# Reordering the first ten projection jobs of a hybrid decoder block, and two more jobs as seven block products

## The chip, the cores and the metric

The kernel runs on one core of a Trainium2 chip. The metric is the device time of one execution in microseconds (us), less being better. TensorE is called PE, VectorE DVE, ScalarE ACT, GpSimd POOL; SP issues most DMAs. PEld is PE's loading of stationary operands, which overlaps its matmuls.

## The reference, cut to what matters

One layer, 256 tokens, width 2048, float32. Cut to the matrix products:

```python
h = rms_norm(x, norm_mix_pre)
p, q, k, v, g_lr, r, gate_logits = split(h @ w_in)          # 1024 1024 1024 2048 16 2048 4096 columns
y_a = pool_mixer(p, w_pool, pool_scale) @ w_branch_a
log_a = log_sigmoid(g_lr @ w_gate_up + b_gate) / 16
o = gla_chunked(q, k, v, log_a)                             # 4 heads, chunks of 64 tokens
o = rms_norm(o, gla_norm) * silu(r)
y_b = o @ w_branch_b
gates = sigmoid(gate_logits + b_branch_gates)
x = x + rms_norm((gates[0] * y_a + gates[1] * y_b) @ w_out, norm_mix_post)
h = rms_norm(x, norm_ffn_pre)
f = (silu(h @ w_ffn_gate) * (h @ w_ffn_up)) @ w_ffn_down    # 5632 columns in between
x = x + rms_norm(f, norm_ffn_post)
```

## The kernel before, in words

**Jobs and steps.** All weight products are a list of 68 jobs, written by `plan()` (L63). A job makes 512 columns of one product for all 256 tokens (two tiles of 128 tokens). Its name is a kind and a number: p0 and p1 are the columns of p, r0 to r3 those of r (r0 also holds the 16 columns of g_lr), and so on; down (2,1) is the second 512 columns of the third part of w_ffn_down, which has 12 tiles of 128 rows where the other jobs have 16 (or 8, for branch a). A plain job goes through its rows in steps of two such tiles. For each step SP loads 512 KB (L334), ACT rounds the weights to a first part `wh` (L343) and DVE computes the rest `wl` (L347). Activations are kept in the same two parts. PE then multiplies three times for each tile of rows and each tile of tokens: first part by first part, first by rest, rest by first (L381 to L383 with 512 columns each; L365 to L367 where the output is wanted transposed, for p, q and k).

**Block jobs.** Where the last value that `plan()` yields is true, the first eight tiles of rows (a 1024 x 512 block) are multiplied with seven products in place of eight: the block is cut into 2 x 2 blocks of 512 x 256, and sums of them are multiplied with sums of the activations' blocks. The seven products are called q1, r5, q6, q7 (these four may run early) and q2, q4, r3. Each has four tiles of rows and one tile of tokens: 12 matmuls of 256 columns (L441 to L443). The sums cost DVE three adds of 128 x 1024 (L402, L404, L406) and POOL one adding DMA (L413); every product has its own `wh` (ACT, L417) and `wl` (DVE, L421) of 128 x 1024. ACT copies running sums out of PSUM (L445, L450, L452) and DVE subtracts (L453). The rest of the rows goes in steps as in a plain job, but as two matmuls of 256 columns instead of one of 512. The activations' sums come from `combine` (L247 on), whose pieces are run as background work.

**What sets the order.** `merged` (L297) weaves the four early products of a block job between the last units of the job ahead of it. A scheduler then places the instructions in each engine's queue when the program is built; each queue runs in order. The limits are pools: four buffers each for `wh` and `wl` (BUFS), three for loaded rows (RAWS), three for blocks of 1 MB (BLOCKS), and eight tiles of 512 columns in PSUM, called banks here. Four (`acc`) hold two jobs' outputs. The other four (`tr`) serve transposes and small products; a block job takes two of them for its running sums (`j.a`, `j.c` in `Part.multiply`, L432), and r0, with its 528 columns, takes two for the whole job beside two of `acc` (`j.extra` in `Step.multiply`, L350).

**Work that hangs on these jobs.** When p0 and p1 end, DVE runs the pooling (L540 to L561) and PE small products with w_pool (L570). When an r job ends, ACT takes silu of it and stores it to DRAM (L586 to L591, `r_done`). r0 also starts the gate chain: the weights of the gate (L603 to L608), the product (L630, L631), then Abs, Exp and Ln on ACT (L636, L639, L643), each over two tiles of 128 x 1024, with a subtraction on DVE (L644). Exp and Ln and silu need other tables in ACT (ACT_TABLE_LOAD). When k1 ends, the levels of the gated attention begin as background work beside the jobs a0 to a3 and v0. At the end of the kernel the third part of down is fed by `f2`, whose third group is transposed on PE (L204) right after up10 and split into `f22h` (ACT, L240) and `f22l` (DVE, L241).

Where rows of an order are shown below, the lines of the changed kernel stand one higher than here from L71 on.

Of the kernel before, what the change touches and what calls it, by code (L numbers as in the profile page):

```python
# [22 lines left out]
RANK = 16  # L23
# [3 lines left out]
CW = 512  # L27
# [26 lines left out]
OFF_P, OFF_Q, OFF_K, OFF_V, OFF_G, OFF_R, OFF_GA = 0, 1024, 2048, 3072, 5120, 5136, 7184  # L54
# [8 lines left out]
def plan():  # L63

    kt = D // P
    for kind, off, order in [("p", OFF_P, (0, 1)), ("r", OFF_R, (1, 2, 3, 0)), ("q", OFF_Q, (0, 1)), ("k", OFF_K, (0, 1))]:
        for i in order:
            low = kind == "r" and i == 0
            yield (kind, i, "w_in", 0, kt, OFF_G if low else off + i * CW, CW + RANK if low else CW,
                   kind == "r" and i > 1)  # L70
    for n in range(4):  # L71
        yield "a", n, "w_branch_a", 0, kt // 2, n * CW, CW, False
    for n in range(4):
        yield "v", n, "w_in", 0, kt, OFF_V + n * CW, CW, n > 0
    for n in range(8):
        yield "gates", n, "w_in", 0, kt, OFF_GA + n * CW, CW, n != 3
    for n in range(4):
        yield "b", n, "w_branch_b", 0, kt, n * CW, CW, n in (1, 3)
    for n in range(4):
        yield "out", n, "w_out", 0, kt, n * CW, CW, n < 3  # L80
    chunks = DFF // CW
    for part in range(3):
        ms = range(part * 4, min(part * 4 + 4, chunks))
        for m in ms:
            yield "gate", m, "w_ffn_gate", 0, kt, m * CW, CW, m > 0
            yield "up", m, "w_ffn_up", 0, kt, m * CW, CW, m > 0
        for n in range(4):
            yield "down", (part, n), "w_ffn_down", part * 16, 4 * len(ms), n * CW, CW, (part, n) not in ((2, 1), (2, 3))


def packed(name, w):

    import numpy as np

    out = []
    for _, _, which, k0, kt, c0, width, fast in plan():
        if which != name:
            continue
        rows = w[0, k0 * P:(k0 + kt) * P, c0:c0 + width].reshape(kt, P, width)
        if fast:  # L100
            for b in range(2):
                blocks = rows[b * 4:b * 4 + 4].reshape(4, P, 2, HW)
                out.append(blocks.transpose(2, 1, 0, 3).ravel())
            rows = rows[4 * FAST:]
        out.append(rows.reshape(-1, GK, P, width).transpose(0, 2, 1, 3).ravel())
    return np.concatenate(out)
# [3 lines left out]
def tile_hybrid_block(ctx: ExitStack, tc: tile.TileContext, *aps):  # L110
# [925 lines left out]
    for kind, n, name, k0, kt, c0, width, fast in plan():  # L1036
        jobs.append(Job(source[name], at[name], kt, width, fast, **kinds[kind](n)))
        at[name] += kt * P * width
# [132 lines left out]
```

## Time and profile before

| | |
|---|---|
| median of 3 runs (lowest, highest) | 1462.31 us (1461.0, 1462.92) |
| the profiled execution | 1462.98 us, its span 1461.2 us |
| PE busy | 1441.4 us (99%) |
| DVE busy | 1230.7 us (84%) |
| ACT busy | 905.0 us (62%) |
| POOL busy | 70.5 us (5%) |
| DMA | 315.50 MB, mean 216 GB/s |
| granted PE clock | 0.999 |

The span runs from the first to the last instruction; the time holds 1.78 us more around it. Busy shares are averages over stages with different limits. PE's records overlap, as matmuls are pipelined: what a matmul costs in a stream is the distance from its start to the next one's.

### The profile page before, as it was taken

To read this page: it belongs to the slowest core of one execution; us is meant where nothing else is said; L and a number is where in the kernel's file an instruction comes from. 1 tells how busy PE (TensorE), PEld (TensorE's weight loads), DVE (VectorE), ACT (ScalarE), POOL (GpSimd) and SP (SyncE) were. 2 spreads that over 40 slices of the span, in tenths; PEclk is the share of its full clock that TensorE was granted. 3 is DMA by queue.
4 is the path that set the end of the run, shared out by engine and by line. 5 is a ranking of instruction groups with operands and counts; after the bars stand their busy time and mean duration, and the time that the engine had idled before them with its cause. 6 is when DMAs were issued, how large, how long until landed. Compare 5 with 4: busy or idle time off the path is not lost.

```text
span 1461.2 us, 27921 instructions
## 1 busy us (share of the span) xinstructions
PE 1441.4 (99%) x11344; PEld 1380.4 (94%) x11344; DVE 1230.7 (84%) x1382; ACT 905.0 (62%) x1183; POOL 70.5 (5%) x95
## 2 busy tenths in 40 slices
PE   8999999999999999999999999999999999999997
PEld 8999999889999999999978999999999999999986
DVE  6785568898998997799778899988889899889986
ACT  6465735556775665566557666666666666666654
POOL 2000000000100000000000000000000000000000
PEclk9999999999999999999999999999999999999999
DMA  8746566726768578649854767777776777777644
GB/s 291 259 136 219 194 211 213 234 90 214 225 201 275 183 251 265 216 150 292 271 169 165 219 221 228 219 227 236 231 223 215 225 230 226 231 238 229 203 166 145
DMA packets 89345, 315.50 MB, mean 216 GB/s; under 512 B 10188, under 2 KB 10912, under 8 KB 88960
## 3 DMA queue, kind: packets, MB, share of 16 engines
q1 hardware_dynamic: 77616, 278.89, 55.8%
q0 software_dynamic: 8304, 29.11, 10.5%
q10 hardware_dynamic: 3296, 5.71, 1.1%
q8 instruction: 89, 1.46, 0.4%
q14 instruction: 40, 0.33, 0.1%
HBM read 284.84 MB, written 4.19 MB: 198 GB/s over the span
## 4 chain that ended last, share of the span: by engine, by line
PE 83%; DVE 8%; issue 3%; DMA 2%; ACT 2%; SPq 0%; POOL 0%; DVEq 0%; ACTq 0%; POOLq 0%
PE acc L381 15%; PE acc L383 15%; PE acc L382 15%; PE ac L441 5%; PE ac L442 5%; PE ac L443 5%; PE acc L443 4%; PE acc L442 4%; PE acc L441 4%; PE acc L367 3%; PE acc L366 3%; PE acc L365 3%; DVE wl L421 2%; DVE wl L347 2%; DMA raw<-in_w_in_dram 2%
## 5 line engine op out<-in xcount | busy, mean ns | idle before, releaser
L343 ACT ACTIVATE wh<-raw 128x1024 fp32r<-128x1024 f32 (+1 forms) x332 | 351.4, 1059 | 285.7 <-PE acc L383 122.3
L347 DVE TENSOR_TENSOR wl<-raw,wh 128x1024 fp32r<-128x1024 f32 (+1 forms) x332 | 405.6, 1223 | 104.4 <-ACT wh L343 101.6
L421 DVE TENSOR_TENSOR wl<-blocks,wh 128x1024 fp32r<-128x1024 f32 x329 | 399.4, 1221 | 76.9 <-ACT wh L417 75.2
L417 ACT ACTIVATE wh<-blocks 128x1024 fp32r<-128x1024 f32 x329 | 346.0, 1059 | 152.6 <-PE acc L383 64.0
L441 PE MATMUL ac<-wh,x 128*128 128x256 f32 x420 | 116.8, 278 | 0.4 <-ACT wh L417 0.4
L442 PE MATMUL ac<-wl,x 128*128 128x256 f32 x420 | 116.2, 277 | 0.0
L443 PE MATMUL ac<-wh,x 128*128 128x256 f32 x420 | 116.1, 277 | 0.0
L382 PE MATMUL acc<-wl,h22h 128*128 128x256 f32 (+1 forms) x336 | 95.3, 284 | 1.6 <-DVE wl L347 1.6
L381 PE MATMUL acc<-wh,h22h 128*128 128x256 f32 (+1 forms) x336 | 95.8, 285 | 0.0
L381 PE MATMUL acc<-wh,h23h 128*128 128x256 f32 (+1 forms) x336 | 94.7, 282 | 0.5 <-ACT wh L343 0.5
L383 PE MATMUL acc<-wh,h22l 128*128 128x256 f32 (+1 forms) x336 | 94.8, 282 | 0.0
L383 PE MATMUL acc<-wh,h23l 128*128 128x256 f32 (+1 forms) x336 | 94.7, 282 | 0.0
L382 PE MATMUL acc<-wl,h23h 128*128 128x256 f32 (+1 forms) x336 | 94.6, 282 | 0.0
L413 POOL DMA_DIRECT2D blocks<-blocks x47 | 40.7, 866 | 883.0 <-DVE blocks L402 154.6
L441 PEld LDWEIGHTS ac<-wh,x 128*128 128x128 f32 x420 | 78.8, 188 | 1.1 <-ACT wh L417 0.6
L442 PEld LDWEIGHTS ac<-wl,x 128*128 128x128 f32 x420 | 78.9, 188 | 0.5
L443 PEld LDWEIGHTS ac<-wh,x 128*128 128x128 f32 x420 | 78.9, 188 | 0.0
L382 PEld LDWEIGHTS acc<-wl,h22h 128*128 128x128 f32 x336 | 63.1, 188 | 2.9 <-DVE wl L347 2.4
L382 PE MATMUL acc<-wl,h2h 128*128 128x256 f32 (+2 forms) x224 | 65.1, 291 | 0.4 <-DVE wl L347 0.4
L381 PE MATMUL acc<-wh,h2h 128*128 128x256 f32 (+2 forms) x224 | 65.1, 291 | 0.0
L383 PE MATMUL acc<-wh,h2l 128*128 128x256 f32 (+2 forms) x224 | 64.9, 290 | 0.0
L382 PE MATMUL acc<-wl,h3h 128*128 128x256 f32 (+2 forms) x224 | 64.7, 289 | 0.0
(549 smaller groups left out, 4614.9 us busy)
## 6 DMA issues: line engine op xcount, KB each, us to landing
raw<-in_w_in_dram SPq DMA_DIRECT2D x120, 512.0 KB, 4.2
blocks<-in_w_in_dram SPq DMA_DIRECT2D x48, 512.0 KB, 4.5
raw<-in_w_ffn_gate_dram SPq DMA_DIRECT2D x48, 512.0 KB, 4.4
raw<-in_w_ffn_up_dram SPq DMA_DIRECT2D x48, 512.0 KB, 4.3
raw<-in_w_ffn_down_dram SPq DMA_DIRECT2D x48, 512.0 KB, 4.4
blocks<-blocks POOLq DMA_DIRECT2D x47, 512.0 KB, 5.8
blocks<-in_w_ffn_gate_dram SPq DMA_DIRECT2D x40, 512.0 KB, 4.3
blocks<-in_w_ffn_up_dram SPq DMA_DIRECT2D x40, 512.0 KB, 4.4
```

The source lines that it names most:

```text
L343: act.activation(self.hi, self.raw, AF.Copy)
L347: dve.tensor_tensor(self.lo, self.raw, f32(self.hi), op=ALU.subtract)
L365: pe.matmul(dst, wh, ah, start=first and c % 2 == 0, stop=False)
L366: pe.matmul(dst, wl, ah, start=False, stop=False)
L381: pe.matmul(ps, ah, hi[:, i, cs], start=first and begins, stop=False, skip_group_check=loose)
L382: pe.matmul(ps, ah, lo[:, i, cs], start=False, stop=False, skip_group_check=loose)
L383: pe.matmul(ps, al, hi[:, i, cs], start=False, stop=last and ends, skip_group_check=loose)
L417: act.activation(self.hi, self.src, AF.Copy)
L421: dve.tensor_tensor(self.lo, self.src, f32(self.hi), op=ALU.subtract)
L441: pe.matmul(dst, ah, wh, start=i == 0 and p in ("q1", "r5"), stop=False, skip_group_check=True)
L442: pe.matmul(dst, ah, wl, start=False, stop=False, skip_group_check=True)
L443: pe.matmul(dst, al, wh, start=False, stop=i == 3 and p in EARLY, skip_group_check=True)
```

## The change

Two rules of `plan()` change. The first ten jobs were p0 p1 r1 r2 r3 r0 q0 q1 k0 k1; now they are p0 p1 r0 r1 q0 r2 q1 r3 k0 k1, and r1 becomes a block job as r2 and r3 are. In down's third part the second job, down (2,1), becomes a block job too; the last, down (2,3), stays plain. The packing of the weights in DRAM follows the same plan on the host.

```diff
-    for kind, off, order in [("p", OFF_P, (0, 1)), ("r", OFF_R, (1, 2, 3, 0)), ("q", OFF_Q, (0, 1)), ("k", OFF_K, (0, 1))]:
-        for i in order:
-            low = kind == "r" and i == 0
-            yield (kind, i, "w_in", 0, kt, OFF_G if low else off + i * CW, CW + RANK if low else CW,
-                   kind == "r" and i > 1)
+    first = {"p": OFF_P, "r": OFF_R, "q": OFF_Q, "k": OFF_K}
+    for kind, i in zip("pprrqrqrkk", (0, 1, 0, 1, 0, 2, 1, 3, 0, 1)):
+
+        low = kind == "r" and i == 0
+        yield (kind, i, "w_in", 0, kt, OFF_G if low else first[kind] + i * CW, CW + RANK if low else CW,
+               kind == "r" and i > 0)
...
-            yield "down", (part, n), "w_ffn_down", part * 16, 4 * len(ms), n * CW, CW, (part, n) not in ((2, 1), (2, 3))
+            yield "down", (part, n), "w_ffn_down", part * 16, 4 * len(ms), n * CW, CW, (part, n) != (2, 3)
```

**PE, the early product r5 of the first block r job.** Before, that job is r2, and its r5 (into the running sum `ac_128_933`) stands between the two small products with w_pool, with half of r1 (`acc_112`, `acc_113`) still ahead:

```order
L383 MATMUL acc_113_833<-wh_118_871,h2l_127 128x512
L570 MATMUL tr_137_974<-qt_120_887,scr_136_972 128x256 [waits DMAHW1_49,DVE_49]
L570 MATMUL tr_137_974<-qt_120_887,scr_136_972 128x256 x3
L441 MATMUL ac_128_933<-wh_121_897,x_74_557 128x256 [waits Activation_49]
L442 MATMUL ac_128_933<-wl_122_899,x_74_557 128x256 [waits DVE_49]
L443 MATMUL ac_128_933<-wh_121_897,x_75_558 128x256
```

Now it is r1, and its r5 (into `ac_129_980`) stands behind the last matmuls of r0, whose four banks are `acc_111`, `acc_112`, `tr_113` and `tr_114`:

```order
L384 MATMUL tr_113_831<-wh_145_1098,h3l_128 128x264
L382 MATMUL acc_112_830<-wh_145_1098,h3h_124 128x264
L383 MATMUL acc_112_830<-wl_146_1100,h3h_124 128x264
L384 MATMUL acc_112_830<-wh_145_1098,h3l_128 128x264
L382 MATMUL tr_114_832<-wh_145_1098,h3h_124 128x264
L383 MATMUL tr_114_832<-wl_146_1100,h3h_124 128x264
L384 MATMUL tr_114_832<-wh_145_1098,h3l_128 128x264
L442 MATMUL ac_129_980<-wh_122_932,x_74_557 128x256 [waits Activation_49]
L443 MATMUL ac_129_980<-wl_123_934,x_74_557 128x256
```

r5 has moved to the end of the job ahead of it, and its first matmul waits for ACT: the instruction that it waits for is ACT's silu of `tr_113`, whose bank `ac_129` takes over.

**DVE, down's third part.** Before, these rows follow the last product of down (2,0), which is `wl_2287`; `wl_2290` is its last step, `wl_2294` and `wl_2298` are the first two steps of the plain job (2,1), `wl_2300` is the early q1 of (2,2), and `ff0`, `ff1` are the outputs of (2,0):

```order
L421 TENSOR_TENSOR wl_2287_16392<-blocks_2248_16093,wh_2286_16390 128x1024
L347 TENSOR_TENSOR wl_2290_16410<-raw_2288_16406,wh_2289_16408 128x1024
L241 TENSOR_TENSOR f22l_15308<-tr_2291_16412,f22h_15304 128x512
L241 TENSOR_TENSOR f22l_15308<-tr_2295_16449,f22h_15304 128x512
L347 TENSOR_TENSOR wl_2294_16447<-raw_2292_16443,wh_2293_16445 128x1024
L347 TENSOR_TENSOR wl_2298_16472<-raw_2296_16468,wh_2297_16470 128x1024
L421 TENSOR_TENSOR wl_2300_16488<-blocks_2258_16179,wh_2299_16486 128x1024
L997 SCALAR_TENSOR_TENSOR ff0_10852<-acc_2264_16206,rstd2_1223_8686,ff0_10852 128x512
L997 SCALAR_TENSOR_TENSOR ff1_10854<-acc_2265_16207,rstd2_1223_8686,ff1_10854 128x512
```

Now `wl_2296` is the last product of (2,0); `blocks_2263` and `blocks_2292` are the blocks of (2,1), `wl_2304` and `wl_2310` its q6 and q7; `wl_2308` and `wl_2313` are the two steps of (2,0):

```order
L422 TENSOR_TENSOR wl_2296_16515<-blocks_2256_16201,wh_2295_16513 128x1024
L403 TENSOR_TENSOR blocks_2263_16255<-blocks_2263_16255,blocks_2292_16467 128x1024
L242 TENSOR_TENSOR f22l_15416<-tr_2298_16520,f22h_15412 128x512
L242 TENSOR_TENSOR f22l_15416<-tr_2305_16548,f22h_15412 128x512
L422 TENSOR_TENSOR wl_2304_16546<-blocks_2263_16255,wh_2303_16544 128x1024
L405 TENSOR_TENSOR blocks_2263_16255<-blocks_2263_16255 128x1024
L348 TENSOR_TENSOR wl_2308_16573<-raw_2306_16569,wh_2307_16571 128x1024
L422 TENSOR_TENSOR wl_2310_16589<-blocks_2263_16255,wh_2309_16587 128x1024
L348 TENSOR_TENSOR wl_2313_16607<-raw_2311_16603,wh_2312_16605 128x1024
L454 TENSOR_TENSOR acc_2301_16529<-ac_2300_16528,u_2314_16621 128x256
```

The steps of (2,0), whose matmuls read `f22h` and `f22l`, have moved behind four early products of (2,1), and two block sums have come in between.

**ACT, the gate chain.** Before, Abs (L636), Exp (L639) and Ln (L643) stand among the `wh` of plain jobs:

```order
L636 ACTIVATE S0_1881<-P0_1879 128x1024
L639 ACT_TABLE_LOAD
L639 ACTIVATE S0_1881<-S0_1881 128x1024
L343 ACTIVATE wh_263_1965<-raw_262_1963 128x1024
L636 ACTIVATE S1_1882<-P1_1880 128x1024
L343 ACTIVATE wh_266_1996<-raw_265_1994 128x1024
L639 ACTIVATE S1_1882<-S1_1882 128x1024
L643 ACT_TABLE_LOAD
```

Now they stand behind r1's silu (L590) and among the `wh` of q0 (L344) and of r2's early products (L418):

```order
L590 ACTIVATE scr_185_1430<-acc_131_982,rstd0_55_440 128x512
L344 ACTIVATE wh_187_1436<-raw_186_1434 128x1024
L592 DMA r11_1432<-scr_185_1430 128x512
L640 ACT_TABLE_LOAD
L640 ACTIVATE S0_1275<-S0_1275 128x1024
L418 ACTIVATE wh_191_1467<-blocks_141_1058 128x1024
L640 ACTIVATE S1_1276<-S1_1276 128x1024
L344 ACTIVATE wh_194_1498<-raw_193_1496 128x1024
L644 ACT_TABLE_LOAD
```

The chain has moved from plain jobs to the job that carries r2's early products; the silus of r2 and r3 now come after it, and ACT's queue holds nine table loads instead of seven. From k0 to up10 PE's queue is the same as before, and the other queues differ in a few places that lie one or two rows apart and in one more table load at the first level of the attention.

## Rows read from the trace of the kernel before

**Rows 1.** The page: busy time (share of the span) and instructions of each engine.
```profile
PE 1441.4 (99%) x11344; PEld 1380.4 (94%) x11344; DVE 1230.7 (84%) x1382; ACT 905.0 (62%) x1183; POOL 70.5 (5%) x95
```
**Rows 2.** PE's waits: who waited for whom: us in total, times, longest.
```profile
PE acc L382 <- DVE wl L347: 2.0, 3, 0.9
...
PE acc L381 <- ACT h20h L243: 0.8, 3, 0.4
PE acc L381 <- ACT f22h L240: 0.8, 1, 0.8
PE acc L383 <- DVE f22l L241: 0.6, 1, 0.6
...
PE ac L441 <- ACT wh L417: 0.4, 1, 0.4
```
**Rows 3.** PE's timeline: start, us, instruction, count [idle before]; 22 matmuls, then 12.
```profile
69.67 0.39 PE L383 MATMUL acc<-wh,h1l 128*128 128x512 f32 x1
...
74.47 0.39 PE L383 MATMUL acc<-wh,h1l 128*128 128x512 f32 x1
74.70 0.28 PE L441 MATMUL ac<-wh,h0h 128*128 128x256 f32 x1
...
75.95 0.28 PE L443 MATMUL ac<-wh,h0l 128*128 128x256 f32 x1
```
**Rows 4.** PE's timeline at the early products of r3.
```profile
104.16 0.39 PE L381 MATMUL acc<-wh,h2h 128*128 128x256 f32 x2
105.00 0.38 PE L441 MATMUL ac<-wh,x 128*128 128x256 f32 x1 [0.45 <-ACT wh L417]
105.22 0.28 PE L382 MATMUL acc<-wl,h2h 128*128 128x256 f32 x1
```
**Rows 5.** PE's timeline at the first step of down (2,0).
```profile
1392.38 0.28 PE L441 MATMUL acc<-wh,f21h 128*128 128x256 f32 x1
...
1393.79 1.04 PE L204 MATMUL tr<-ident,scr 128*128 128x128 f32 x8
1395.63 0.39 PE L381 MATMUL acc<-wh,f22h 128*128 128x256 f32 x1 [0.80 <-ACT f22h L240]
...
1396.10 0.28 PE L382 MATMUL acc<-wl,f22h 128*128 128x256 f32 x1
1397.01 0.38 PE L383 MATMUL acc<-wh,f22l 128*128 128x256 f32 x1 [0.63 <-DVE f22l L241]
```
**Rows 6.** ACT's timeline where r0 ends.
```profile
153.34 0.27 ACT L586 ACTIVATE glow<-acc,rstd 128x16 f32<-128x16 f32 x1 [0.76 <-PE acc L383]
153.51 0.46 ACT L589 ACTIVATE scr<-acc,rstd 128x248 f32<-128x248 f32 x1
153.86 0.48 ACT L589 ACTIVATE scr<-tr,rstd 128x264 f32<-128x264 f32 x1
```
**Rows 7.** ACT's timeline in the gate chain.
```profile
166.19 1.28 ACT L639 ACT_TABLE_LOAD   x1
167.49 1.06 ACT L639 ACTIVATE S<-S 128x1024 f32<-128x1024 f32 x1
168.46 1.04 ACT L343 ACTIVATE wh<-raw 128x1024 fp32r<-128x1024 f32 x1
```
**Rows 8.** DVE's timeline: a stretch without idle time, and the last part of down.
```profile
78.79 1.22 DVE L347 TENSOR_TENSOR wl<-raw,wh 128x1024 fp32r<-128x1024 f32 x1
79.92 1.22 DVE L404 TENSOR_TENSOR blocks<-blocks 128x1024 f32<-128x1024 f32 x1
81.06 1.22 DVE L421 TENSOR_TENSOR wl<-blocks,wh 128x1024 fp32r<-128x1024 f32 x1
...
1387.29 0.43 DVE L453 TENSOR_TENSOR acc<-ac,u 128x256 f32<-128x256 f32 x1
1387.62 1.22 DVE L421 TENSOR_TENSOR wl<-blocks,wh 128x1024 fp32r<-128x1024 f32 x1
```
**Rows 9.** Busy time by stretch: us, PE PEld DVE ACT POOL, clock, DMA share, GB/s.
```profile
63.60:94.50 30.90, 30.90 (x163) 26.56 (x162) 28.35 (x45) 16.74 (x22) 0.95 (x1) 1.00 0.46 133
131.00:154.20 23.20, 23.20 (x194) 23.20 (x193) 10.48 (x9) 10.24 (x13) 0.00 (x0) 1.00 0.70 232
154.20:199.50 45.30, 45.30 (x396) 45.05 (x395) 29.91 (x35) 29.12 (x33) 1.92 (x2) 1.00 0.62 206
```
**Rows 10.** The same over 1387.3 to 1436.6 us: the row of sums.
```profile
sum 49.30, PE 47.86 PEld 44.43 DVE 40.45 ACT 28.18 POOL 1.13; mean PE 11.97 PEld 11.11 DVE 10.11 ACT 7.04 POOL 0.28
```
**Rows 11.** DMA issues: count, KB each, median us from issue to landing.
```profile
raw<-in_w_ffn_down_dram SPq DMA_DIRECT2D x48, 512.0 KB, 4.4
blocks<-blocks POOLq DMA_DIRECT2D x47, 512.0 KB, 5.8
...
wgu<-in_w_gate_up_dram ACTq DMA_DIRECT2D x3, 64.0 KB, 2.0
```

## The prediction

> **What bounds the kernel now.** I read the page's busy line first. PE is busy for 99% of the span, DVE for 84% [rows 1]. That alone does not say that PE is the bound everywhere, so I read PE's waits next: the longest entry of PE waiting for DVE's `wl` is 2.0 us in three waits, the others are below 1 us [rows 2]. So PE's stream is the path, and the kernel gets shorter by what leaves that stream and longer by each new hole in it. DVE is the engine to watch for holes: while r1 and the early products of r2 ran, from 63.6 to 94.5 us, DVE was busy 28.35 of 30.90 us, but only 10.48 of 23.20 in r0 and 29.91 of 45.30 in q0 and q1 [rows 9]. In the last part of down, from 1387.3 to 1436.6 us, it was busy 40.45 of 49.30 [rows 10].
>
> All sums below are made against the profiled execution, 1462.98 us, which is 0.67 us above the median of the runs shown, 1462.31. About 0.2% of that, 2.9 us, is what a measurement of this kernel can tell from no change.
>
> **PE's stream: -3.0 us.** Matmuls of 512 columns start 4.80 us / 21 = 0.2286 us apart, those of 256 columns 1.25 / 11 = 0.1136 [rows 3]. A plain r job is 8 steps x 2 x 2 x 3 = 96 of the long ones, 21.95 us. As a block job it is 7 x 12 = 84 short ones and 4 steps x 24 = 96 short ones, 180 in all, 20.45 us: -1.50. Down (2,1) falls from 6 x 12 = 72 long ones, 16.46 us, to 84 + 48 = 132 short ones, 15.00 us: -1.46. Moving a job past another costs PE nothing in itself.
>
> **What the two jobs cost the others.** Seven products stand in place of four steps, so each of the two jobs gives ACT and DVE three more pieces of 128 x 1024, DVE three block sums and two subtractions, and POOL one adding DMA. On DVE a piece takes 1.13 to 1.14 us from start to start and a subtraction 0.33 [rows 8]: 6 x 1.135 + 2 x 0.33 = 7.5 us a job. The bytes loaded stay the same; SP's queue issues 512 KB pieces as before, whose landing takes 4.4 us, and the adding DMA 5.8 us [rows 11].
>
> **A hole that goes near 105 us: -0.7 us.** r3's q6 had to wait for its `wh` there: two matmuls from 104.16 would have ended by 104.39, the next began at 105.00, and the one after it 0.22 instead of 0.11 us later [rows 4]. DVE was late because two block jobs followed each other while the pooling was still being worked off. Now r3's early products lie between steps of q1, which are 24 matmuls long, and the pooling is long over.
>
> **The wait that r1's r5 gets: +1.4 us.** r5's running sum takes over a bank of r0, so its first matmul waits for ACT's silu of that bank, and r5 stands directly behind r0's last matmul. Everything on PE waits with it. ACT cannot start on r0 before the last matmul into `acc_111`, the tenth from the end: some 1.05 us before r0's stream ends, and it is there at about 0.9, as u and `wh` of r1's s4 stand ahead. Then come the copy of g_lr, 0.17 to the next start, a table load, 1.30, silu of 248 columns, 0.35, and silu of 264 columns, 0.48 [rows 6, 7]: 2.3 us, so r5 is let go 1.4 us after it could run. Bounds: 0.9 if ACT starts the moment it can and the table load overlaps something, 2.8 if ACT is a piece of 1.06 us later. What is queued behind r5 on PE waits too; on DVE the two subtractions of r1 wait for r5, but they have 3 us to spare. For the gate's weights behind them, the chain of a memset, a DMA of 2.0 us [rows 11] and two pieces ends some 2.5 us before PE wants them; that is their cover.
>
> The ScalarE page of the Trainium skill ("ScalarE: Activation LUTs", section "What ACT_TABLE_LOAD costs") says that a switch of tables costs 1283 ns and a drain of some 1380 ns, 2.66 us together, and asks that work be grouped by table, which this change undoes for silu. The load is 1.28 us here too, but the trace shows the next instruction 0.02 us behind it [rows 7], so I price a switch at 1.30; by the page r5's wait would be 2.8 us.
>
> **Small lateness in the new front: +0.6 us (0 to 2).** DVE's order puts a block sum ahead of the `wl` of r0's s5, and r5 no longer stands before that step on PE. Summing DVE's rows from 58.2 us on, with the prices above, `wl` is there 0.3 us after PE wants it: +0.3. In q0, the two Exp, two Ln and the silus of r1 lie between the `wh` of q0 and of r2's early products. Two table loads at 1.30 and some ten pieces at 0.95 to 0.97 [rows 7] from r1's end bring Ln's end to 12.6 us after it; then a piece of 1.2 and a block sum lead to the `wl` of q0's s5, wanted 16.4 us after r1's end: I get 0.3 us late, +0.3. Two more table loads lie in ACT's idle time (q0 and q1 had 29.12 of 45.30 us of it busy [rows 9]) and cost nothing.
>
> **The end: -1.8 us and +2.7 us.** Before, down (2,0) had its first step as second unit, right behind the transposes of up10's last group. The eight transposes begin at 1393.79, at 0.11 us each PE was free at 1394.66, the step began at 1395.63; then from 1396.10 to 1397.01 it waited again for `f22l` [rows 5]: 0.97 + 0.80 = 1.8 us. Now q4, r3 and three early products of (2,1) stand ahead of that step, 5 x 1.36 = 6.8 us of cover: both waits go.
>
> What is late next is DVE. It enters with a lead: (2,0)'s q2 began on PE at 1392.38, while its `wl` was done at 1388.84 [rows 5, 8]. From 1387.62 on I count DVE's order up to the `wl` of (2,2)'s q6: 21 pieces at 1.135, six of half size at 0.60, two outputs at 0.66, three subtractions at 0.33, 29.7 us, so it is done at 1417.4. PE without a hole gets there after 12 units of 12 matmuls, two of 24 and the transposes, 16.3 + 5.4 + 0.9 = 22.6 us after 1392.38, at 1415.0, and wants `wl` 0.1 us later. So PE loses 2.3 us by then, mainly at r5 and q6 of (2,2); with 0.4 us for pieces that wait for ACT, +2.7. Behind that point the plain job (2,3) gives DVE its slack back. Lower bound 0.5, if DVE keeps more of its lead; upper bound the whole 7.5 us, if none of DVE's idle time can be used.
>
> **Sum.** -3.0 - 0.7 + 1.4 + 0.6 - 1.8 + 2.7 = -0.8: 1462.2 us for the profiled execution, **1461.5 us** for the median.
>
> **The rivals.** *The holes stay small.* DVE keeps its lead in down (+0.5), the front is not late (0), r5's wait is 0.9: -3.0 - 0.7 + 0.9 - 1.8 + 0.5 = -4.1, 1458.2. For it: DVE has 8.85 us of idle time in the end [rows 10], more than the 7.5 it gets. Against it: products of 1.36 us on PE need 1.14 us of DVE each, and the block sums and outputs come on top. Chance 0.22.
>
> *Slower: DVE becomes the bound of down's third part.* Weight pieces are made at most four units ahead of PE, and an early product has PE's time for 12 matmuls alone, so DVE's idle time may be of no use; then all 7.5 us appear on PE: -0.8 + 4.8 = +4.0, 1466.3. It decides where the `wl` of (2,1)'s s4 comes more than 2 us after PE's end of q6. For it: in three block jobs of 15 us in a row DVE has 12 pieces, two subtractions and two outputs in two passes each, 16.8 us a job. Against it: the third of them is followed by a plain job, and the first enters with the lead of 3.5 us. Chance 0.12.
>
> *Slower: a table switch costs far more than its row.* At 2.7 us a switch, r5's wait doubles (+1.4) and the two loads in q0 add 2.8 to the lateness of q0's s5: +3.4, 1465.7. The rows show nothing behind a load but 0.02 us [rows 7]: chance 0.03. This is the case that the ScalarE page of the Trainium skill would make.
>
> That the block jobs are not made where the change puts them is excluded by the order shown.
>
> **How the numbers follow.** The forecast has a chance of 0.63. It lies within 0.2%, the first rival is faster by 4.1 us, the other two are slower by over 2.9. So faster 0.22, same 0.63, slower 0.15. The range reaches down to the first rival's time and up to near the two slower ones, which leaves out about 2 in 10: 1458.0 to 1465.5. The forecast's own range is 1459.5 to 1464.5.
>
> **What would show it.** Right: r1 takes 180 matmuls of 256 columns; one hole of about 1.4 us directly before r1's r5, ended by ACT's silu; no hole at r3's q6; no wait for `f22h`; some 2 to 3 us of PE waiting for `wl` in (2,1) and the early products of (2,2). Wrong: holes in r2 or r3, DMA landings that end waits in down's third part, or PE waiting for DVE in down for more than 5 us or less than 1.

## The result and the profile after

The changed kernel takes 1464.91 us in the median of 12 runs (1463.81 to 1467.08), the kernel before 1462.16 beside it (12 runs). The ratio is 1.0019, 95% interval 1.0011 to 1.0027: a loss of 2.75 us where 0.8 us of gain was forecast. The time lies inside the range on record, at its upper end; the sign was wrong.

The profiled execution of the changed kernel took 1464.67 us, its span is 1462.9. Its busy line, beside [rows 1]:

```profile
PE 1441.2 (99%) x11488; PEld 1386.5 (95%) x11488; DVE 1244.8 (85%) x1398; ACT 917.2 (63%) x1199; POOL 72.6 (5%) x97
```

PE has 144 matmuls more and is busy for as long as before, though the short matmuls of two jobs were to save 3 us. DVE has 14 us more and ACT 12, as counted (7.5 a job on DVE).

PE's waits in the changed kernel (who waited for whom, us in total, times, longest), beside [rows 2]:

```profile
...
PE acc L383 <- DVE wl L348: 1.6, 2, 0.9
PE ac L442 <- ACT scr L590: 1.5, 1, 1.5
PE acc L382 <- ACT wh L344: 1.1, 2, 0.6
...
PE ac L442 <- ACT wh L418: 0.6, 1, 0.6
PE acc L367 <- DVE wl L348: 0.5, 1, 0.5
...
PE ac L442 <- DVE f22l L242: 0.4, 1, 0.4
...
PE acc L442 <- DVE acc L454: 0.3, 1, 0.3
```

The forecast wait is there (silu, L590, 1.5 us), the wait for `f22h` is gone, that for `f22l` is 0.4 and in another place. But the new waits together do not make the loss. To see where it lies I cut both spans at the same places of the program, by the start of the first matmul of a job:

| from ... to | before | after | difference |
|---|---|---|---|
| start to the first r job | 63.72 | 63.62 | -0.1 |
| first r job to a0 | 179.33 | 182.71 | +3.4 |
| a0 to down (2,0), its q1 | 1132.21 | 1130.89 | -1.3 |
| down (2,0), its q1, to down (2,3) | 61.36 | 61.09 | -0.3 |
| the last job and what is behind it | 24.6 | 24.6 | 0.0 |

The third line is no work of the change: PE's instructions there are the same, and over the runs below that leave its banks as they are this stretch took from 1131.0 to 1132.4 us, with the old front and with the new. So the change costs some 3.4 us in the first ten jobs and gives 0.3 back in down. The first of these stretches, and k0 with k1 inside it, by windows: the stretch, its length, busy time of PE, PEld, DVE, ACT, POOL with instruction counts (a window also counts what overlaps its ends), granted clock, DMA share, GB/s. The kernel before:

```profile
63.72:243.05 179.33, 178.88 (x1444) 174.05 (x1443) 123.39 (x141) 98.70 (x112) 3.18 (x4) 1.00 0.58 190
199.53:243.05 43.52, 43.52 (x386) 43.52 (x385) 28.05 (x30) 18.41 (x18) 0.00 (x0) 1.00 0.59 197
```

The changed kernel:

```profile
63.62:246.33 182.71, 180.39 (x1529) 179.25 (x1528) 130.17 (x148) 105.14 (x120) 3.72 (x4) 1.00 0.57 187
201.09:246.33 45.24, 45.24 (x387) 45.24 (x386) 26.56 (x27) 20.19 (x21) 0.00 (x0) 1.00 0.66 214
```

The second line of each is the surprise. k0 and k1 are 384 matmuls of 256 columns in both kernels, in the same order, with no idle time in either and the clock at its upper level (1.00). They take 43.52 us before and 45.24 after: 0.1133 and 0.1178 us from start to start. PE's timeline of the changed kernel where r3 ends and k0 begins (start, us, instruction, count):

```profile
200.41 0.28 PE L382 MATMUL acc<-wh,h3h 128*128 128x256 f32 x1
...
201.09 0.28 PE L366 MATMUL acc<-h0h,wh 128*128 128x256 f32 x1
...
202.28 0.28 PE L367 MATMUL acc<-h0h,wl 128*128 128x256 f32 x1
```

Six matmuls of r3 take 0.68 us, the ten of k0 behind them 1.19. From the first matmul of k0 on PE goes 4% slower, with nothing waited for, for 45 us. I call this PE's pace. Sorting all distances between successive starts on PE from the first r job to a0 by size gives the whole: distances up to 0.13 us for 256 columns (0.245 for 512) are pace, what is above is a hole. Matmul columns at the fast pace (0.1133 us for each 256): -1.4; holes: 3.1 before, 5.0 after, +1.9; pace: 0.9 before, 3.8 after, +2.9. Sum +3.4.

### The profile page after: what moved, and what is told of

The parts are those of the page before. It is cut to its first block, busy times and chain, and to the rows that moved or that the text cites. A ratio compares the mean times of both kernels' runs of the same rounds, so it can differ in the third digit from the quotient of the medians.

```text
span 1462.9 us, 28244 instructions
## 1 busy us (share of the span) xinstructions
PE 1441.2 (99%) x11488; PEld 1386.5 (95%) x11488; DVE 1244.8 (85%) x1398; ACT 917.2 (63%) x1199; POOL 72.6 (5%) x97
## 3 DMA queue, kind: packets, MB, share of 16 engines
q8 instruction: 90, 1.47, 0.4%
## 4 chain that ended last, share of the span: by engine, by line
PE 85%; DVE 6%; issue 3%; ACT 2%; DMA 2%; SPq 0%; POOL 0%; DVEq 0%; ACTq 0%; POOLq 0%
PE acc L382 15%; PE acc L383 15%; PE acc L384 15%; PE ac L442 5%; PE ac L443 5%; PE ac L444 5%; PE acc L442 4%; PE acc L444 4%; PE acc L443 4%; PE acc L368 2%; PE acc L367 2%; PE acc L366 2%; DVE wl L422 2%; DMA raw<-in_w_in_dram 2%; DVE wl L348 1%
## 5 line engine op out<-in xcount | busy, mean ns | idle before, releaser
L344 ACT ACTIVATE wh<-raw 128x1024 fp32r<-128x1024 f32 (+1 forms) x324 | 343.0, 1059 | 265.1 <-PE acc L384 109.2
L422 DVE TENSOR_TENSOR wl<-blocks,wh 128x1024 fp32r<-128x1024 f32 x343 | 416.0, 1220 | 79.0 <-ACT wh L418 77.1
L348 DVE TENSOR_TENSOR wl<-raw,wh 128x1024 fp32r<-128x1024 f32 (+1 forms) x324 | 395.3, 1222 | 87.0 <-ACT wh L344 84.2
L418 ACT ACTIVATE wh<-blocks 128x1024 fp32r<-128x1024 f32 x343 | 360.9, 1059 | 165.4 <-PE acc L384 65.8
L442 PE MATMUL ac<-wh,x 128*128 128x256 f32 x432 | 120.0, 278 | 1.5 <-ACT scr L590 1.5
L443 PE MATMUL ac<-wl,x 128*128 128x256 f32 x432 | 119.7, 277 | 0.0
L444 PE MATMUL ac<-wh,x 128*128 128x256 f32 x432 | 119.6, 277 | 0.0
L442 PEld LDWEIGHTS ac<-wh,x 128*128 128x128 f32 x432 | 81.1, 188 | 2.1 <-ACT scr L590 1.7
L444 PEld LDWEIGHTS ac<-wh,x 128*128 128x128 f32 x432 | 81.2, 188 | 0.0
L384 PE MATMUL acc<-wh,h3l 128*128 128x256 f32 (+2 forms) x232 | 66.0, 285 | 0.0
```

The costliest lines, as they stand in the source:

```text
L344: act.activation(self.hi, self.raw, AF.Copy)
L348: dve.tensor_tensor(self.lo, self.raw, f32(self.hi), op=ALU.subtract)
L384: pe.matmul(ps, al, hi[:, i, cs], start=False, stop=last and ends, skip_group_check=loose)
L418: act.activation(self.hi, self.src, AF.Copy)
L422: dve.tensor_tensor(self.lo, self.src, f32(self.hi), op=ALU.subtract)
L442: pe.matmul(dst, ah, wh, start=i == 0 and p in ("q1", "r5"), stop=False, skip_group_check=True)
```

## The experiments

Two theories. **A**: PE has two paces for the same matmuls, a state that lasts until something in its stream disturbs it, and the new order of jobs puts q1's first steps, k0 and k1 into the slower one. **B**: the loss is the new holes, and the pace is a matter of the single execution.

**e1_front, e2_order, e3_r1, e4_down** take the change apart.

```diff
 e1_front (of the changed kernel)
-... (part, n) != (2, 3)
+... (part, n) not in ((2, 1), (2, 3))
 e2_order: as e1_front, and
-... kind == "r" and i > 0
+... kind == "r" and i > 1
 e3_r1 (of the kernel before)
-... kind == "r" and i > 1
+... kind == "r" and i > 0
 e4_down (of the kernel before)
-... (part, n) not in ((2, 1), (2, 3))
+... (part, n) != (2, 3)
```

> The new order with r1 as a block job, but down (2,1) plain as before. Theory A (pace): matmuls of 256 columns start either 113.3 or 117.8 ns apart, the state lasts over many jobs, and the new order, in which q and k jobs follow block jobs, puts q1, k0 and k1 into the slower one. Then k0 and k1 run at 117.8 again, the stretch from r0 to a0 is about 183 us as in the changed kernel, and the time is 2.5 to 3.5 us above before. Theory B (waits): the holes that the change makes are the loss, and the pace is a matter of the single execution. Then k0 and k1 are as likely at 113.3, and the time is 1 to 2 us above before.

> The new order alone: r1 and down (2,1) stay plain. Theory A: q1, k0 and k1 at 117.8 ns although no job has changed its form, 2 to 3 us above before. Theory B: no wait before r1's r5, since there is none; the hole at r3's q6 gone (-0.7), q0's s5 late (+0.7): the time of before, within 0.5 us.

> The old order p0 p1 r1 r2 r3 r0 q0 q1 k0 k1 with r1 as a block job; down as before. Theory A: q0 to k1 follow the plain job r0 as before and stay at 113.3 ns; r1 saves 1.3 us of matmuls, and its early products fall into p1, where DVE also has the pooling: new holes of 1 to 3 us there; 0 to 2 us above before. Theory B: the same holes, so the same time, and k0 and k1 at either pace.

> Old order, r1 plain, only down (2,1) as a block job. Both theories: in down's third part the two waits for f22h and f22l go (-1.8), the early products of (2,2) wait for their weights (+2), matmuls -1.3: 0 to 1 us below before. Theory A: everything ahead of down paced as before (113.3 in q0 to k1). Theory B: paced as it happens.

Against before: e1_front 1.0023 (1.0014 to 1.0033), e2_order 1.0012 (1.0003 to 1.0021), e3_r1 1.0038 (1.0025 to 1.0050), e4_down 0.9997 (0.9988 to 1.0006). So the front alone makes the loss (+3.4 us) and down gives 0.4 back, which alone can't be told from nothing; together they are the change's +2.75 within the intervals. More than half of the front's loss, 1.8 us, is the order alone, which changes no matmul. That figure is a mean over runs that spread widely: three of e2_order's 11 runs (1461.64, 1461.95 and 1462.27 us) lie where the kernel before lies, and with one profile of each kernel it stays open whether these ran at the faster pace. Its windows of k0 and k1 (e2_order):

```profile
199.95:245.18 45.23, 45.23 (x386) 45.23 (x385) 26.55 (x27) 20.20 (x21) 0.00 (x0) 1.00 0.64 215
```

and the same of e4_down, which has the old order:

```profile
198.84:242.36 43.52, 43.52 (x386) 43.52 (x385) 28.03 (x30) 18.39 (x18) 0.00 (x0) 1.00 0.60 199
```

k0 and k1 took 45.23 in e1_front too, and 43.52 in e3_r1: the slower pace in each run with the new order, the faster in each with the old one. B falls here, as far as the pace is concerned. Its share in the holes stays: e1_front is 1.6 us behind e2_order, of it 1.0 in the first ten jobs (182.03 against 181.06), where r1's block products save 1.4 us of columns at the fast pace and bring 2.4 us of holes.

e3_r1 lost far more than expected, +5.6 us, and elsewhere. Its PE waits begin with

```profile
PE tr L204 <- DMA x<-in_x_dram: 7.1, 1, 7.1
```

against 2.7 us in three waits before. SP's queue shows why:

```profile
1.18 0.89 SPq L185 DMA_DIRECT2D x<-in_x_dram  x2
2.11 0.91 SPq L1069 DMA_DIRECT2D blocks<-in_w_in_dram  x2
3.06 0.43 SPq L334 DMA_DIRECT2D raw<-in_w_in_dram  x1
```

With a block job as third, its 1 MB block is loaded at 2.11 us, ahead of three quarters of x, which p0 waits for. So r1 as a block job wants a plain job between p1 and itself, which the new order has.

**e5_nudge and e7_r0first** ask what the pace belongs to.

```diff
 e5_nudge (of the changed kernel, in the steps of q and k)
...
+if i == 0:
+    for n in NUDGE.get((j.label, g), ()):
+        pe.matmul(bank()[:, :n], ah[:, :P] if n > T else hi[:, 0, :P],
+                  hi[:, 0, :n] if n > T else ah[:, :n], start=True, stop=True)
 e7_r0first (of the changed kernel)
-zip("pprrqrqrkk", (0, 1, 0, 1, 0, 2, 1, 3, 0, 1))
+zip("pprrrrqqkk", (0, 1, 0, 1, 2, 3, 0, 1, 0, 1))
```

> The changed kernel with extra matmuls of PE, whose result nobody reads, ahead of some steps of q1, k0 and k1, each into a free bank of tr: one of 128 columns ahead of q1's first step and of k0's first step, then one of 64 (k0's third step), one of 256 (k0's fifth), two of 128 (k0's seventh), one of 512 (k1's first), three of 128 (k1's third), one of 192 (k1's fifth), one of 32 (k1's seventh). Theory A (the pace is a state of PE's stream that lasts until something disturbs it): at some of these places the spacing changes between 117.8 and 113.3 ns and stays there until the next one. Theory C (the pace belongs to the job: its operands' or its banks' addresses, which the extra matmuls leave alone): q1's first steps, k0 and k1 stay at 117.8 ns throughout. The extra matmuls cost some 1.3 us themselves.

> The changed kernel with the order p0 p1 r0 r1 r2 r3 q0 q1 k0 k1: the same jobs in the same forms, no q or k job between r jobs. Theory A1 (what sets the slower pace is a q or k job that starts behind block products or plain r matmuls of 512 columns): q0 to k1 all at 117.8 ns, 384 x 2 matmuls x 4.5 ns = 3.4 us of pace; r5's wait stays; the late weights near r3's q6 come back (0.7): 3 to 5 us above before. Theory A2 (the switching to and fro between the two forms sets it): q0 to k1 at 113.3 ns, time within 2 us of before.

e5_nudge took 1466.27 us in one run. Its windows from k0's first step to its third, on to k1's first, to k1's third, to k1's seventh, to a0:

```profile
201.56:207.33 5.77, 5.77 (x52) 5.77 (x51) 2.45 (x2) 2.90 (x4) 0.00 (x0) 1.00 0.87 256
207.33:224.13 16.80, 16.80 (x150) 16.80 (x149) 7.54 (x7) 6.37 (x6) 0.00 (x0) 1.00 0.67 236
224.13:230.01 5.88, 5.88 (x51) 5.84 (x50) 5.85 (x8) 4.56 (x5) 0.00 (x0) 1.00 0.54 178
230.01:241.37 11.36, 11.36 (x102) 11.36 (x101) 8.04 (x9) 4.25 (x4) 0.00 (x0) 1.00 0.56 186
241.37:247.14 5.77, 5.77 (x52) 5.77 (x50) 2.76 (x3) 2.12 (x2) 0.00 (x0) 1.00 0.55 182
```

With their extra matmuls taken off, the 48 regular ones of the first line are 0.118 us apart, the 144 of the second 0.1133 but for the first few, then 0.118, 0.1133 and 0.118 again. The pair of 128 and 64 columns turned the pace to fast, 512 to slow, three of 128 to fast, 32 to slow; 128 at the start of q1 and k0 left it slow, and 256, two of 128 and 192 left it fast. The same operands and banks, in one job, run at either pace: theory C falls, and A stands.

e7_r0first takes 1.0058 (1.0046 to 1.0071). In this order the kernel's output is wrong, and which part of the chain behind the first jobs it breaks stays open; so I use its spacing alone, on the assumption (not shown) that this does not hang on the values. From q0 to a0, 768 matmuls:

```profile
161.84:252.29 90.45, 90.45 (x770) 90.45 (x769) 50.34 (x50) 37.17 (x37) 0.00 (x0) 1.00 0.61 204
```

That is 0.1178 us each, all four jobs at the slower pace, as A1 said and A2 did not: taking turns is not needed for it. But a block job ahead is not enough either, so A1 is not the rule. In the changed kernel q0 stands behind the block job r1 and runs at the faster pace, while q1 behind r2 runs at the slower one. The end of r1 (134 matmuls of 256 columns) and the first 96 of q0, then the end of r2 (132) and the first 96 of q1:

```profile
99.09:114.90 15.81, 15.81 (x136) 15.81 (x135) 10.78 (x16) 8.71 (x11) 1.80 (x2) 1.00 0.93 266
114.90:125.79 10.89, 10.89 (x98) 10.89 (x97) 6.07 (x6) 10.83 (x12) 0.00 (x0) 1.00 0.56 195
143.25:158.22 14.97, 14.97 (x135) 14.97 (x133) 11.61 (x13) 7.97 (x8) 0.00 (x0) 1.00 0.74 250
158.22:169.53 11.31, 11.31 (x99) 11.31 (x98) 5.79 (x6) 6.14 (x7) 0.00 (x0) 1.00 0.65 217
```

These are 0.1180 and 0.1134 us each, then 0.1134 and 0.1178. So it is in every trace of the new order, and in e7_r0first: a q or k job that comes directly behind the matmuls of an r job starts at the other pace than they ended at. This is what the traces show; no run was made to test it as a rule.

**e8_pace, e9_slow and e10_best** were to price the pace, each with extra matmuls like those above (64 columns ahead of k0's second step in the changed kernel; 32 there in the kernel before; 64 at seven places in e4_down).

> The changed kernel with one extra matmul of 64 columns, whose result nobody reads, ahead of k0's second step; all other instructions stand in the same order. Theory A (the pace is a state of PE's stream and costs time): from that place to k1's end matmuls of 256 columns start 113.3 ns apart instead of 117.8; 15 steps x 24 x 4.5 ns = 1.6 us less, a0's long matmuls 0.1 less, the extra matmul 0.1 more: 1.6 us below the changed kernel, about 1.2 us above before. Rival (the time lost in pace is made up later, or the loss is the holes alone): the time of the changed kernel, within 0.5 us.

> The kernel before with one extra matmul of 32 columns ahead of k0's second step; nothing else differs. Theory A: the matmuls behind it go to 117.8 ns, as 32 columns did in k1, and stay there to a0: 1.6 to 1.9 us above before, though no wait is added. Rival: the state is set by the order of jobs alone and the extra matmul does nothing here: the time of before, within 0.3 us.

> Old order, r1 plain, down (2,1) as a block job, and one extra matmul of 64 columns at seven places where the traces show 117.8 ns for a long stretch: ahead of v1's q2, of q4 of v2, v3 and gates0, of the seventh step of gates4 and of the sixth of b1 and b3. Theory A: if 64 columns turn the pace there as in k0, 0.2 to 0.4 us less at each, about 1 us in all beside the 0.4 of down: 1.4 us below before. If the size that turns it is another in these jobs, some of the stretches stay at 117.8 and the time is that of down alone, 0.4 us below before.

All three were slower than expected: 1.0046 (1.0032 to 1.0060), 1.0050 (1.0038 to 1.0063), 1.0025 (1.0015 to 1.0035). In e8_pace the 64 columns did not turn the pace: the 360 matmuls behind them took 42.5 us, 0.118 each. In e9_slow the 32 columns did, and k0 to a0 took 45.23 us, but much more was lost behind it. PE where v2's q1 begins in e9_slow:

```profile
348.46 0.27 PE L205 MATMUL tr<-ident,scr 128*128 128x128 f32 x1
349.26 0.39 PE L446 MATMUL ac<-wh,h0h 128*128 128x256 f32 x1 [0.52 <-DVE scr L801]
```

The extra matmul had taken one turn of the four tr banks, so every later tile stood one bank further on, and the block jobs' running sums, whose banks are fixed, now took over banks that DVE still had to read: four such waits of 0.68 us in v2, v3, gates0 and gates1, and more behind. These runs price a shift of the banks with the pace, and e10_best besides left v1's stretch slow. So they were made again with the rotation kept:

```diff
+kept = banks["at"]
 pe.matmul(bank()[:, :n], ...
+banks["at"] = kept
```

**e11_slow2** gives the kernel before the slower pace, **e12_pace2** the changed kernel the faster one, with the pair of e5_nudge.

> As e9_slow, but the extra matmul of 32 columns in k0 leaves the rotation of the four tr banks as it was, so that later tiles stand in the same banks as before (in e9_slow v2's, v3's, gates0's and gates1's q1 each waited 0.68 us for a bank, which the kernel before does not). Theory A: k0's second step to k1's end at 117.8 ns and nothing else: 1.6 to 2.0 us above before. Rival: the loss of e9_slow was the extra matmul's place in the queue and not the pace or the banks: 5 us or more above before again.

> The changed kernel with one extra matmul of 128 columns ahead of k0's first step and one of 64 ahead of k0's third, as in e5_nudge, whose pair turned the pace there; the rotation of the tr banks stays. Theory A: k0's third step to k1's end at 113.3 ns, 14 x 24 x 4.5 ns = 1.5 us less, the extra matmuls 0.25 more, a0 0.15 less: 1.2 to 1.5 us below the changed kernel, 1.0 to 1.8 above before. Rival: the loss of the change is in its holes alone: no faster than the changed kernel.

e11_slow2: 1.0012 (1.0004 to 1.0021), 1463.51 against 1462.01 us. One matmul of 32 columns, whose result nobody reads, costs 1.5 us. Its timeline and its windows ahead of it and behind:

```profile
201.49 0.28 PE L374 MATMUL acc<-h0l,wh 128*128 128x256 f32 x1
201.61 0.18 PE L366 MATMUL tr<-h0h,wh 128*128 128x32 f32 x1
201.63 0.36 PE L372 MATMUL acc<-h0h,wh 128*128 128x256 f32 x1
```

```profile
198.89:201.49 2.60, 2.60 (x25) 2.60 (x24) 2.56 (x4) 1.06 (x1) 0.00 (x0) 1.00 0.78 232
201.49:244.12 42.63, 42.63 (x364) 42.63 (x363) 25.58 (x27) 17.28 (x17) 0.00 (x0) 1.00 0.57 188
```

Before it 23 distances make 2.60 us, 0.113; behind it 361 matmuls make 42.63, 0.118, up to a0 and without idle time.

e12_pace2: 1.0014 (1.0005 to 1.0023), 1463.63 us, so 1.6 above before where the change itself is 2.75 above. Its windows of k0's first two steps with the 128 columns, and from there to a0, 337 regular matmuls and one of 64 columns:

```profile
200.76:206.36 5.60, 5.60 (x50) 5.60 (x49) 2.45 (x2) 2.90 (x4) 0.00 (x0) 1.00 0.91 271
206.36:244.74 38.38, 38.38 (x341) 38.38 (x340) 23.99 (x25) 17.32 (x17) 0.00 (x0) 1.00 0.63 213
```

The second is 0.114 each. With the two useless matmuls k0 and k1 take 43.98 us, 1.3 less than the 45.24 of the changed kernel, which is what A said. The time is lower too, by 1.1 us, but the intervals of the two kernels overlap, so this half is shown by the trace and not by the time. The other half is shown by both: in e11_slow2 k0 and k1 take 45.23 us, 1.7 more than before, and the time is 1.5 us longer, clear of noise. So the pace of k0 and k1 costs time, some 1.5 us, without a wait; the rival of e11_slow2, 5 us or more, is out.

**e6_copy** takes away r5's wait on the silu.

```diff
 e6_copy (of the changed kernel, r_done)
+if n == 0:
+    dve.tensor_copy(s[:, out[1][1]], out[1][0])
+    out[1] = s[:, out[1][1]], out[1][1]
 for ps, c in out:
     act.activation(s[:, c], ps, AF.Silu, scale=rz(t))
```

> The changed kernel, but DVE copies r0's two banks of tr out of PSUM at once, and ACT's silu of that part reads the copy in SBUF; so r5's bank comes free without the table load. My theory of the wait (ACT's table load and silus, 1.47 us idle before r5): the hole falls to 0.3 to 0.6 us, the wait of r1's q2 for the subtractions (0.47) stays or goes with it; the time falls by 1.0 to 1.6 us against the changed kernel, to about 1.3 us above before. Rival: r5 then waits for its own weights or another bank as long: no change.

It failed: 1.0039 (1.0026 to 1.0053). PE where r0 ends in e6_copy:

```profile
91.98 0.27 PE L205 MATMUL tr<-ident,glow 128*16 128x128 f32 x1
93.42 0.28 PE L205 MATMUL tr<-ident,glow 128*16 128x128 f32 x1 [1.17 <-ACT glow L587]
93.45 0.36 PE L442 MATMUL ac<-wh,x 128*128 128x256 f32 x1
```

r5 no longer waits for the silu, but the scheduler has put the two transposes of g_lr ahead of it, and the second of them waits for a copy that stands behind the same table load in ACT's queue. The wait has changed its name and kept 1.2 us of its length. The gate chain moved with it, and in q0 r2's q6 then waited 1.8 us for its `wh`. Right behind that, in the profiled execution, the granted clock stood at 0.50, the lower of its two levels (1.2 GHz), after PE had been busy for 2.21 of 4.00 us:

```profile
130.00:134.00 4.00, 2.21 (x18) 2.00 (x18) 4.00 (x5) 3.99 (x5) 0.96 (x1) 0.98 0.12 34
134.00:137.20 3.20, 3.20 (x17) 3.20 (x17) 3.02 (x3) 1.17 (x2) 0.00 (x0) 0.50 0.40 147
```

There 15 matmuls of 256 columns started 0.213 us apart, which cost 1.5 us more than at 0.1133. So part of this run's loss is a slower clock behind a wait. That r5's wait can be removed at no cost is not shown; in both orders what PE waits for there stands behind the table load.

No run beat the kernel before by more than its interval. e4_down, the change's last part alone, is the nearest.

## Why the prediction was right and wrong

**The step that failed** is "Moving a job past another costs PE nothing in itself", with the prices under it, 0.1136 for each matmul of 256 columns. The price was read from one stretch [rows 3]. In its place the runs showed a second pace of 0.1178, and that the order decides which one holds: +2.9 us in the front, of it 1.7 in k0 and k1, where the forecast had 0. It could have been read before. p1 in the trace of the kernel before, three whole steps of 24 matmuls:

```profile
40.67:49.15 8.48, 8.48 (x74) 8.48 (x73) 8.30 (x17) 4.06 (x4) 0.00 (x0) 1.00 0.93 307
```

8.48 us for 72 is 0.1178, without idle time: the slower pace, in a stretch that I did not measure. What the order does with it could not have been read there; that it is a free term of 4% over all 68 jobs could.

**"The others are below 1 us"**, of PE's waits, was misread. The trace before also has 2.7 us for `x` and 1.1 us for `scr` (L176). Both lie ahead of the first r job, so no term of the sum hangs on them.

**r1's columns, -1.5.** Much of it did not come, for the same reason. Of r1's 180 matmuls those from r5 and q2 on, 144, ran at 0.1178; at the rows' prices that makes 36 x 0.1136 + 144 x 0.1178 = 21.05 us against 21.95, so 0.9 was saved.

**r5's wait, +1.4.** Right in place and cause, and near in size: 1.47 us idle, 1.7 us counted by starts. ACT's timeline where r0 ends in the changed kernel, which answers to [rows 6]:

```profile
91.87 0.27 ACT L587 ACTIVATE glow<-acc,rstd 128x16 f32<-128x16 f32 x1 [0.24 <-PE acc L384]
92.15 1.28 ACT L590 ACT_TABLE_LOAD   x1
93.45 0.47 ACT L590 ACTIVATE scr<-acc,rstd 128x248 f32<-128x248 f32 x1
93.81 0.47 ACT L590 ACTIVATE scr<-tr,rstd 128x264 f32<-128x264 f32 x1
94.18 0.28 ACT L587 ACTIVATE glow<-acc,rstd 128x16 f32<-128x16 f32 x1
```

and PE's, with the step behind r5:

```profile
94.34 0.39 PE L442 MATMUL ac<-wh,x 128*128 128x256 f32 x1 [1.47 <-ACT scr L590]
...
96.55 0.39 PE L442 MATMUL acc<-wh,h1h 128*128 128x256 f32 x1 [0.31 <-DVE acc L454]
```

The chain is the one that was summed: copy, table load, two silus, then r5 after 1.47 us. The load takes 1.28 and the next instruction starts 0.02 behind it, so the rival of a switch at 2.7 us did not come. By the Trainium skill ("ScalarE: Activation LUTs", section "What ACT_TABLE_LOAD costs") a drain of some 1380 ns comes on top of the load, 2.66 us for a switch; this trace does not agree, as the load begins 0.01 us behind the copy's end and the silu 0.02 us behind the load's.

**"They have 3 us to spare"**, of r1's two subtractions, was wrong. q2 stands directly behind r5 and writes the same tile as the subtraction that waits for r5: another 0.31 idle, 0.47 with the slower start behind it.

**Small lateness in the front, +0.6.** r0's s5 was not late. q0's s5 waited 0.54 for its `wl`, where 0.3 was summed; in e1_front, with the same front, it did not wait at all, and 1.4 us were lost there in e5_nudge. It stands on the edge that the sum put it on.

**The hole at r3's q6, -0.7.** Gone, as forecast; it is there in the runs with the old order (0.6 lost in e4_down and e11_slow2).

**The end, -1.46 - 1.8 + 2.7.** Forecast -0.6, measured -0.3 in the stretch; by the same sorting as above, columns -1.4, holes +1.4, pace -0.3. The mechanism was right. PE in down's third part of the changed kernel:

```profile
1400.33 0.38 PE L442 MATMUL ac<-wh,f20h 128*128 128x256 f32 x1 [0.43 <-DVE f22l L242]
```

```profile
1419.45 0.38 PE L442 MATMUL ac<-wh,fx 128*128 128x256 f32 x1 [0.64 <-ACT wh L418]
1420.39 0.51 PE L382 MATMUL acc<-wh,f22h 128*128 128x256 f32 x2 [0.56 <-ACT wh L344]
```

The lateness falls on (2,2)'s q6 and the step behind it, at 1419.45 and 1420.39; the profile ends the waits with ACT's `wh`, the piece that each `wl` is made from. With 0.3 at r5 and the slower starts behind the holes, 2.1 us are lost there, where 2.3 were summed. The waits at (2,0)'s first step [rows 5] fell from 1.77 to 0.26 us, and one came that was not summed: (2,1)'s q1 takes over the bank that `f22l` is still read from, 0.43 idle. That is r5's kind of wait once more, and it was in the order to be seen.

**The rivals.** DVE as the bound of down's third part (+4.8 there) did not come: e4_down is 0.4 below before. The small holes did not come either. The case that came, a slower PE without a wait, was none of the three.

## What to carry to other kernels

Where PE is the bound, measure the distance between its matmuls in every kind of stretch, not in one, before an edit is priced: a few per cent in that distance over a whole job weigh as much as a wait, and no list of waits shows them. An extra tile in a rotation of banks is not free either: it moves all later tiles, and what takes over a bank next waits for its last reader. After a move, compare stretch by stretch at the same places of the program; here columns and waits together made 0.5 of 3.4 us, and the pace the rest.

## What the runs showed of the hardware that was not expected

Matmuls of 256 columns, back to back, with the granted clock at 1.00 (the upper of its two levels, 2.4 GHz), start 0.1133 or 0.1178 us apart. The same instructions in the same order do either, for tens of us, and the switch comes at a change in the stream: another form of matmul, a small one in between (32 columns to slow in e11_slow2, 64 behind 128 to fast in e12_pace2), or a hole. In a0's matmuls of 512 columns it is 0.2290 before and 0.2335 in the changed kernel, the same 4.5 ns. What the state is inside PE, and by which rule a disturbance turns it, stays open: the same 64 columns left the pace slow in e8_pace. One regularity is seen, that a q or k job directly behind an r job's matmuls takes the other pace than theirs (0.1134 behind 0.1180 and 0.1178 behind 0.1134 in the changed kernel); it was not tested by itself. The pace mostly repeats from execution to execution (k0's first step slow in all five profiles of the new order without a matmul put ahead of it, fast in all six of the old), but p0 and p1, behind the loads of x, came out at either pace.
